# Gate and up products of a SwiGLU layer as Strassen block products, with the hidden tiles kept in DRAM

## The chip, the cores and the metric

The kernel runs on one NeuronCore of a Trainium2 chip. The metric is the device time of one execution, in microseconds (us): the median of three runs.

## The reference

One layer of a hybrid decoder trunk works on 1056 tokens at once: a prompt of 1024 and 32 sample tokens, with shared weights and a model width of 1024. Three token mixers and their output projection come first, then a cross-attention to 256 memory tokens, then the feed-forward part, which is what the change touches:

```python
h = h + mem_attention(rmsnorm(h, W['norm_mem'][l]), mem_k[l], mem_v[l], W['w_mem_q'][l], W['w_mem_o'][l])
u = rmsnorm(h, W['norm_ffn'][l])
h = h + (jax.nn.silu(u @ W['w_ffn_gate'][l]) * (u @ W['w_ffn_up'][l])) @ W['w_ffn_down'][l]
...
y = rmsnorm(h, W['norm_final'])
```

Everything is float32. The hidden width is 2816, 22 tiles of 128 features.

## The kernel before

Activations lie with features on the 128 partitions and tokens along the free side: `h` is eight tiles of 128 x 1056. A main product is done in three passes of float32r matmuls: each operand is split into a high part (a copy rounded to float32r, on ScalarE) and a low part (the rest, a subtraction on VectorE), and `unit` (lines 143 to 153) issues high x high, low x high and high x low for each of `kk` input tiles of 128 features into one PSUM tile of 352 tokens. The tokens are three chunks of 352 (`ch`, `CW`, `NCH`).

TensorE and SyncE (SP, which issues the loads) run in the order of the program text; the order on VectorE (DVE), ScalarE (ACT) and GpSimd (POOL) is made ahead by a scheduler, and each engine then works strictly in that order. Work beside the main products is written as generators: `spawn` starts one, and each `yield n` lets it go on after `n` more half units of main products, counted by `tick` (lines 78 to 95). `strips` (line 120) gives the weight strips in the order of their use, each loaded and split one ahead (`load_split`, `split_into`).

Buffers: `slot` gives one of 28 SBUF tiles of 128 x 1056 values, `slot2` one of 5 more. One PSUM pool, open for the whole kernel, has 3 banks for main products (`mmps`) and 5 for the rest (`smps`).

The work around the change:
- The attention's output product w_o comes in two halves over its input features (`w_o_half`, line 1108): 8 output tiles x 3 chunks x 4 input tiles x 3 matmuls each. As each chunk of the second half leaves PSUM, `residual` adds it to `h` (line 907), `square_into` sums the squares for the norm (ScalarE, then GpSimd at line 221), and `upair` (line 223) writes the high and low part of h times the norm's gain into `u`, 16 tiles.
- `rstd` (line 188) makes the norm's factor per token: sums over features by matmuls with ones, a square root and a Newton step, transposes back onto all partitions (`rbc`). The products don't wait for it, since the factor is applied to their results.
- `hidden` (line 1134) makes a group of 6, 6, 6 or 4 hidden tiles: for each tile and chunk a gate and an up product over 8 input tiles (24 matmuls each), then `evac` (lines 1146 to 1154): gate result x factor, SiLU, up result x factor, their product, and its split into `hh` and `hl`.
- After each of the first three groups the down products over its 6 tiles are added to `h` (lines 1162 to 1167). The last group's down products run over 384, 384 and 288 tokens, each followed by the final norm (`finish`, line 1182) and the store of the output.

## Time and profile before

| what | value |
|---|---|
| runs | 1843.45, 1843.9 and 1845.54 us, median 1843.9 |
| span of the profiled execution, first to last instruction | 1838.8 us |
| instructions | 29217 |
| TensorE, matmuls | 11410, busy 97% of the span |
| VectorE, ScalarE, GpSimd busy | 54%, 38%, 22% |
| DMA | 150.31 MB, mean 82 GB/s |
| mean granted TensorE clock | 0.997 |
| gate and up products | from 1052 us to about 1790, in turns with the down products |

The device time of a run also holds what lies ahead of the first and behind the last instruction; the profiled execution has no separate time of its own on record, so its span stands beside the median of the runs: 5.1 us lie between the two. Busy time of TensorE is the sum of what single matmuls take from their start to their modelled end; successive matmuls overlap, so the distance of their starts tells what one costs in a stream.

### The profile page before, as it was taken

Reading aid. Unit: us, or ns where it says so; the run is one execution under the profiler, and the core shown is the slowest. Engines: PE = TensorE matmul, PEld = TensorE weight load, DVE = VectorE, ACT = ScalarE, POOL = GpSimd, SP = SyncE. Lnnn points to the kernel's source line nnn. Section 1 sums busy time; section 2 is a strip of 40 time slices with the busy share of each in tenths; the row PEclk is TensorE's granted clock in tenths of the full one; section 3 lists DMA queues with packets and bytes.
Section 4 is the critical chain, followed back from the end, with each engine's and each line's share of the span. In section 5 each row is a group of like instructions: output and inputs, shape, how many; then the busy total and the mean of one; then the engine's idle time right before and its main releaser. Section 6 shows DMA issues by size and latency. Waiting matters only on the chain.

```text
span 1838.8 us, 29217 instructions
## 1 busy us (share of the span) xinstructions
PE 1788.8 (97%) x11410; PEld 1739.2 (95%) x11410; DVE 991.9 (54%) x1990; ACT 692.6 (38%) x1403; POOL 412.8 (22%) x516
## 2 busy tenths in 40 slices
PE   8899999999999999999999999999999999999997
PEld 7798888888999999999999999999999999999996
DVE  5888997798745434455575743333333233333345
ACT  6544443577634113355563532211221122211244
POOL 2423557665342222212220400000000000000014
PEclk9999999999999999999999999999999999999999
DMA  9112122341322412234452111111111111111112
GB/s 348 52 60 68 59 57 90 112 134 58 126 84 89 170 58 94 88 121 126 121 180 93 47 47 46 41 48 48 44 46 50 49 36 46 43 52 50 47 47 95
DMA packets 84316, 150.31 MB, mean 82 GB/s; under 512 B 12881, under 2 KB 27857, under 8 KB 84177
## 3 DMA queue, kind: packets, MB, share of 16 engines
q1 hardware_dynamic: 73808, 130.82, 22.2%
q10 hardware_dynamic: 10368, 17.61, 2.7%
q8 instruction: 90, 1.47, 0.3%
q14 instruction: 50, 0.40, 0.1%
HBM read 128.02 MB, written 20.37 MB: 81 GB/s over the span
## 4 chain that ended last, share of the span: by engine, by line
PE 81%; DVE 8%; POOL 3%; issue 3%; ACT 2%; DMA 2%; SPq 0%; ACTq 0%; DVEq 0%; POOLq 0%
PE mm L148 24%; PE mm L149 24%; PE mm L150 24%; DVE cy L498 1%; PE poa L1077 1%; PE pss L1059 1%; POOL seg L570 1%; DVE x L325 1%; PE poz L1008 1%; DVE seg L553 1%; PE pof L688 1%; DVE ul L225 1%; PE pdg L591 1%; PE psa L1008 1%; DVE h L1205 0%
## 5 line engine op out<-in xcount | busy, mean ns | idle before, releaser
L148 PE MATMUL mm<-uh,whi 128*128 128x352 f32 x2016 | 661.7, 328 | 0.8 <-DVE h L907 0.8
L150 PE MATMUL mm<-uh,wlo 128*128 128x352 f32 x2016 | 650.6, 323 | 0.0
L149 PE MATMUL mm<-ul,whi 128*128 128x352 f32 x2016 | 650.6, 323 | 0.0
L148 PEld LDWEIGHTS mm<-uh,whi 128*128 128x128 f32 x2016 | 380.1, 189 | 5.3 <-issue 2.9
L149 PEld LDWEIGHTS mm<-ul,whi 128*128 128x128 f32 x2016 | 380.1, 189 | 2.5
L150 PEld LDWEIGHTS mm<-uh,wlo 128*128 128x128 f32 x2016 | 379.3, 188 | 0.0
L117 ACT ACTIVATE whi<-wraw 128x512 fp32r<-128x512 f32 (+1 forms) x264 | 151.8, 606 | 372.7 <-PE mm L149 340.8
L1218 POOL TENSOR_TENSOR acc_mem<-acc_mem,sq 128x384 f32<-128x384 f32 (+1 forms) x18 | 17.6, 980 | 740.6 <-ACT sq L1216 740.1
L118 DVE TENSOR_TENSOR wlo<-wraw,whi 128x512 fp32r<-128x512 f32 x232 | 158.0, 704 | 18.8 <-ACT whi L117 18.2
L150 PE MATMUL mm<-hh,wlo 128*128 128x352 f32 x432 | 139.9, 324 | 0.0
L148 PE MATMUL mm<-hh,whi 128*128 128x352 f32 x432 | 139.6, 323 | 0.0
L149 PE MATMUL mm<-hl,whi 128*128 128x352 f32 x432 | 139.5, 323 | 0.0
L1151 DVE TENSOR_TENSOR t<-mm,rbc_ffn 128x352 f32<-128x352 f32 x66 | 34.7, 525 | 188.5 <-PE mm L150 188.5
L1167 DVE TENSOR_TENSOR h<-h,mm 128x352 f32<-128x352 f32 x72 | 37.6, 522 | 141.3 <-PE mm L150 141.3
L1153 ACT ACTIVATE hh<-t 128x352 fp32r<-128x352 f32 x66 | 32.9, 498 | 182.1 <-DVE t L1152 182.0
L1149 DVE TENSOR_TENSOR t<-mm,rbc_ffn 128x352 f32<-128x352 f32 x66 | 34.7, 525 | 94.8 <-PE mm L150 94.6
L149 PEld LDWEIGHTS mm<-hl,whi 128*128 128x128 f32 x432 | 81.4, 188 | 0.0
L148 PEld LDWEIGHTS mm<-hh,whi 128*128 128x128 f32 x432 | 81.2, 188 | 0.0
L150 PEld LDWEIGHTS mm<-hh,wlo 128*128 128x128 f32 x432 | 81.1, 188 | 0.0
L952 POOL TENSOR_TENSOR kvlo<-kvraw,kvhi 128x512 fp32r<-128x512 f32 x32 | 41.5, 1296 | 161.3 <-ACT kvhi L951 128.8
L498 DVE SCALAR_TENSOR_TENSOR cy<-raw,cst,cy 128x352 f32<-128x352 f32 (+1 forms) x108 | 72.3, 671 | 7.0 <-ACT cy L496 3.6
L1150 ACT ACTIVATE t<-t 128x352 f32<-128x352 f32 x66 | 32.5, 492 | 109.4 <-DVE t L1149 109.4
(395 smaller groups left out, 3329.3 us busy)
## 6 DMA issues: line engine op xcount, KB each, us to landing
wraw<-w_gu SPq DMA_DIRECT2D x88, 256.0 KB, 2.9
seg<-acs_dram SPq DMA_DIRECT2D x32, 256.0 KB, 3.8
wraw<-w_out SPq DMA_DIRECT2D x32, 256.0 KB, 3.7
kvraw<-kc_d SPq DMA_DIRECT2D x32, 256.0 KB, 2.9
kvraw<-vc_d SPq DMA_DIRECT2D x32, 256.0 KB, 2.8
wraw<-w_down SPq DMA_DIRECT2D x32, 256.0 KB, 2.8
kvw<-w_kv SPq DMA_DIRECT2D x15, 512.0 KB, 7.3
wraw<-w_xbc SPq DMA_DIRECT2D x24, 256.0 KB, 3.1
```

The costliest lines, as they stand in the source:

```text
L117: nc.scalar.activation(hi[:, a:b], raw, AF.Copy)
L118: (second if a else nc.vector).tensor_tensor(lo[:, a:b], raw, hi[:, a:b].bitcast(F32), op=OP.subtract)
L148: nc.tensor.matmul(out, whi[:, a:b], xh[:, cols], start=k == 0, stop=False)
L149: nc.tensor.matmul(out, whi[:, a:b], xl[:, cols], start=False, stop=False)
L150: nc.tensor.matmul(out, wlo[:, a:b], xh[:, cols], start=False, stop=k == kk - 1)
L498: nc.vector.scalar_tensor_tensor(y[:, :n], raw[:, j:j + n], w[j], y[:, :n], op0=OP.mult, op1=OP.add)
L952: eng.tensor_tensor(lo, src, hi.bitcast(F32), op=OP.subtract)
L1008: nc.tensor.matmul(pr, diag[:, k * 512 + b * 2 * ST:k * 512 + (b + 1) * 2 * ST], pair[z][:, k], start=b + k + z == 0, stop=b + k + z == NB ...
L1149: nc.vector.tensor_tensor(t1, pg, rbc[:, ch(c)], op=OP.mult)
L1151: nc.vector.tensor_tensor(t2, pu, rbc[:, ch(c)], op=OP.mult)
L1153: nc.scalar.activation(hh[:, ch(c)], t2, AF.Copy)
L1167: nc.vector.tensor_tensor(h[m][:, ch(c)], h[m][:, ch(c)], p, op=OP.add)
```

## The change

The gate and up products are done by Strassen's scheme with seven block products and shared sums (Winograd's form). The two matrices of a pair of hidden tiles (2 x 128 features) and the two halves of the 1024 input features make the 2 x 2 blocks of the left side; the right side is cut the same way by input features and by tokens: two halves `s` of 528 tokens (`TH`). The tokens of each half are again cut in two quarters of 264 (`HB`), and index `c` (0 or 1) takes one quarter from each half; all of it is done for c = 0 and for c = 1 apart.

- `sides(c)` makes the right-hand sides: the normed tokens times gain and factor, four sums and differences, and the high and low parts of all seven, for four input tiles: 14 `slot` tiles for each c, so all 28. Two products share tiles `x2`, `x3`, `x4`.
- `lefts` loads the strips of a pair of tiles, makes the sums s1 to s4 and splits the seven left-hand sides, in four lists. `ahead_of` prepares none ahead in the first block and two lists ahead later.
- `product` issues 4 input tiles x 3 matmuls of 264 columns. The seven products fall into four PSUM tiles of two banks (`G[0]` to `G[3]`, three buffers); products 0 and 2, 1 and 3, 4 and 6 add up in the same tile, and the partial sum is read in between (`after`). The first gate block and the last up block run all seven products for c = 0 and then for c = 1 (`by_part`); the others run each product for both.
- `gate` and `up` combine the results, apply SiLU and multiply, and the four pieces of two hidden tiles are stored to `hid_dram` on ScalarE's DMA queue.
- The second half of w_o runs over quarters: both halves `s` of c = 0 for all 8 output tiles, then c = 1, with all its weights split once and held (`hold`). Behind c = 0 `sides(0)` is spawned, behind c = 1 `sides(1)`. `h` is stored to `h_dram`.
- The down products come after all hidden tiles. `load_hidden` reads a hidden tile back and splits it (ScalarE and VectorE, 1056 columns), six ahead of the first product and one per output tile after that; `h` is loaded again. Their matmuls stay as they were; the last eight weight strips are loaded behind the third group.
- PSUM is given out by three pools in turn, the second with six banks for `G` and two for the rest.

The diff, cut to its core:

```diff
+TH = T // 2
+HB = TH // 2
...
+        lists += [(w_o[0, m], 512) for m in range(8)]
+        yield from one_ahead(lists, mixers)
...
+    hid_dram = dr.tile([P, FT, T], F32, name="hid_dram")
...
+    def both(t, c):
+        return t.rearrange("p (s t) -> p s t", s=2)[:, :, c * HB:(c + 1) * HB]
...
+    def rstd2(c):
+        pv = smps(name="pv")
+        cuts = [(2 * s + i, s * TH + c * HB + i * P, P) for s in range(2) for i in range(2)]
+        cuts += [(4 + s, s * TH + c * HB + 2 * P, HB - 2 * P) for s in range(2)]
+        for i, a, n in cuts:
+            nc.tensor.matmul(pv[:n, i:i + 1], acc[:, a:a + n], ones[:, :1], start=True, stop=True)
...
+        newton(r, v, q)
+        yield 2
+        for s in range(2):
+            pb = smps(name="pb")
+            a0 = s * TH + c * HB
+            for i, a, n in cuts:
+                if a0 <= a < a0 + HB:
+                    nc.tensor.transpose(pb[:, a - a0:a - a0 + n], r[:n, i:i + 1].to_broadcast([n, P]), ident[:n, :n])
+            nc.scalar.activation(rbc[:, a0:a0 + HB], pb[:, :HB], AF.Copy)
...
+    def sides(c, n0):
+        yield n0
+        yield from rstd2(c)
+        un = {}
+        def normed(k):
+            un[k] = fp.tile([P, 4, HB], F32, tag="ar", name=nm("un"), bufs=4)
+            for j in range(2):
+                nc.scalar.activation(un[k][:, 2 * j:2 * j + 2], both(h[k + 4 * j], c), AF.Copy, scale=cc("gffn", k + 4 * j))
+                (nc.gpsimd if j else nc.vector).tensor_tensor(un[k][:, 2 * j:2 * j + 2], un[k][:, 2 * j:2 * j + 2], both(rbc, c),
+                                                              op=OP.mult)
+        def pair(t, q, n, src):
+            hi = t[:, q * HB:(q + n) * HB].rearrange("p (s t) -> p s t", s=n)
+            lo = t[:, (q + n) * HB:(q + 2 * n) * HB].rearrange("p (s t) -> p s t", s=n)
+            nc.scalar.activation(hi, src, AF.Copy)
+            nc.vector.tensor_tensor(lo, src, hi.bitcast(F32), op=OP.subtract)
+            return [(quarters(t, q + i), quarters(t, q + n + i)) for i in range(n)]
+        normed(0)
+        for k in range(4):
+            if k < 3:
+                normed(k + 1)
+            u4 = un[k]
+            tt = fp.tile([P, 4, HB], F32, tag="as", name=nm("tt"), bufs=2)
+            if k % 2 == 0:
+                first = slot(F32R, "x1")
+            X["B11", k, c] = pair(first, k % 2 * 2, 1, u4[:, 0:1])[0]
+            nc.vector.tensor_tensor(tt[:, 0:2], u4[:, 1::2], u4[:, 0:2], op=OP.subtract)
+            nc.vector.tensor_tensor(tt[:, 2], u4[:, 3], tt[:, 0], op=OP.subtract)
+            nc.vector.tensor_tensor(tt[:, 3], u4[:, 2], tt[:, 2], op=OP.subtract)
+            X["T2", k, c], X["T4", k, c] = pair(slot(F32R, "x2"), 0, 2, tt[:, 2:4])
+            X["B21", k, c], X["B22", k, c] = pair(slot(F32R, "x3"), 0, 2, u4[:, 2:4])
+            X["T1", k, c], X["T3", k, c] = pair(slot(F32R, "x4"), 0, 2, tt[:, 0:2])
...
+    def hold():
+        m = len(held)
+        if m % 2 == 0:
+            hold.at = [(wp if m < 4 else fp).tile([P, DM], F32R, tag=t if m < 4 else "b" + t, name=nm(t), bufs=2) for t in ("whi", "wlo")]
+        hi, lo = (t[:, m % 2 * 512:m % 2 * 512 + 512] for t in hold.at)
+        split_into(w_o[1, m], 512, hi, lo)
+        held.append((hi, lo))
+    hold()
+    for c in range(2):
+        for m in range(8):
+            while len(held) < min(m + 2, 8):
+                hold()
+            for s in range(2):
+                cols = slice(s * TH + c * HB, s * TH + (c + 1) * HB)
+                p = mmps()[:, :HB]
+                unit(p, held[m], op1, cols, 4)
+                nc.vector.tensor_tensor(h[m][:, cols], h[m][:, cols], p, op=OP.add)
+            if m:
+                sq = fp.tile([P, 2, HB], F32, tag="sq2", name=nm("sq"), bufs=2)
+                nc.scalar.activation(sq, both(h[m], c), AF.Square)
+                nc.gpsimd.tensor_tensor(both(acc, c), both(acc, c), sq, op=OP.add)
+            else:
+                nc.scalar.activation(both(acc, c), both(h[m], c), AF.Square)
+            if c:
+                nc.scalar.dma_start(h_dram[:, m, :], h[m])
+        if c == 0:
+            spawn(sides(0, 4))
+    drain()
+    ps_.close()
+    sm_bufs = 2
+    ps_ = ExitStack()
+    ps = ps_.enter_context(tc.tile_pool(name="ps2", bufs=2, space=PSUM, reuse_waits="tile"))
+    spawn(sides(1, 1))
...
+    def lefts(pairs):
+        raws = []
+        def load(i):
+            r = [fp.tile([P, DM], F32, tag="ar", name=nm("ar"), bufs=4, padded_shape=[P, T]) for _ in range(2)]
+            for k in range(2):
+                for t, src in zip(r, pairs[i]):
+                    nc.sync.dma_start(t[:, k * 512:k * 512 + 512], src[:, k * 512:k * 512 + 512])
+            raws.append(r)
+        load(0)
+        for i in range(len(pairs)):
+            (a11, a12), (a21, a22) = [(t[:, :512], t[:, 512:]) for t in raws.pop(0)]
+            if i + 1 < len(pairs):
+                load(i + 1)
+            sa, sb = (fp.tile([P, DM], F32, tag="as", name=nm("as"), bufs=2, padded_shape=[P, T]) for _ in range(2))
+            s1, s2, s3, s4 = sa[:, :512], sa[:, 512:], sb[:, :512], sb[:, 512:]
+            nc.gpsimd.tensor_tensor(s1, a21, a22, op=OP.add)
+            nc.gpsimd.tensor_tensor(s3, a11, a21, op=OP.subtract)
+            nc.vector.tensor_tensor(s2, s1, a11, op=OP.subtract)
+            nc.vector.tensor_tensor(s4, a12, s2, op=OP.subtract)
+            for n, srcs in enumerate(((a11, s2), (a12, s3), (s1, a22), (s4,))):
+                pool, b = (fp, "b") if n % 2 else (wp, "")
+                hi, lo = (pool.tile([P, DM], F32R, tag=b + t, name=nm(t), bufs=2) for t in ("whi", "wlo"))
+                for j, src in enumerate(srcs):
+                    a = slice(j * 512, j * 512 + 512)
+                    nc.scalar.activation(hi[:, a], src, AF.Copy)
+                    nc.vector.tensor_tensor(lo[:, a], src, hi[:, a].bitcast(F32), op=OP.subtract)
+                yield [(hi[:, j * 512:j * 512 + 512], lo[:, j * 512:j * 512 + 512]) for j in range(len(srcs))]
...
+    def ahead_of(gen):
+        got = []
+        for x in gen:
+            got.append(x)
+            while len(got) > lead[0]:
+                yield from got.pop(0)
...
+    PRODUCTS = ("B11", 0, True), ("T2", 1, True), ("B21", 0, False), ("T3", 1, False), ("T1", 2, True), ("T4", 3, True), ("B22", 2, False)
+    NF2 = FT // 2
+    blocks = ahead_of(lefts([(w_gu[j, 2 * f], w_gu[j, 2 * f + 1]) for f in range(NF2) for j in range(2)]))
...
+    def product(i, w, G, c, kk):
+        xb, g, begins = PRODUCTS[i]
+        whi, wlo = w
+        for k in range(kk):
+            a, b = k * P, k * P + P
+            xh, xl = X[xb, k, c]
+            out = G[g][:, c, :HB]
+            nc.tensor.matmul(out, whi[:, a:b], xh, start=begins and k == 0, stop=False, skip_group_check=True)
+            nc.tensor.matmul(out, whi[:, a:b], xl, start=False, stop=False, skip_group_check=True)
+            nc.tensor.matmul(out, wlo[:, a:b], xh, start=False, stop=k == kk - 1, skip_group_check=True)
+        tick()
...
+    def strassen(kk, after, by_part):
+        G = {}
+        if by_part:
+            ws = [next(blocks) for _ in range(7)]
+            for c in range(2):
+                for i in range(7):
+                    g = PRODUCTS[i][1]
+                    if g not in G:
+                        G[g] = ps.tile([P, 2, 512], F32, tag="st", name=nm("st"), bufs=3)
+                    product(i, ws[i], G, c, kk)
+                    after(i, slice(c, c + 1), G)
+                G = {}
+            return
+        for i in range(7):
+            g = PRODUCTS[i][1]
+            if g not in G:
+                G[g] = ps.tile([P, 2, 512], F32, tag="st", name=nm("st"), bufs=3)
+            w = next(blocks)
+            for c in range(2):
+                product(i, w, G, c, kk)
+            after(i, slice(0, 2), G)
...
+        def gate(i, cs, G):
+            m1, u2, u3 = s22[:, cs], s12[:, cs], s21[:, cs]
+            at = lambda g: G[g][:, cs, :HB]
+            vec = nc.vector.tensor_tensor
+            if i == 0:
+                nc.scalar.activation(m1, at(0), AF.Copy)
+            elif i == 1:
+                vec(u2, m1, at(1), op=add)
...
+        strassen(4, gate, f == 0)
+        lead[0] = 2
...
+                nc.gpsimd.tensor_tensor(s22[:, cs], s22[:, cs], m1, op=mul)
...
+        strassen(4, up, f == NF2 - 1)
+        for n, t in enumerate(ga):
+            nc.scalar.dma_start(hid_dram[:, 2 * f + n // 2, n % 2 * TH:(n % 2 + 1) * TH], t.rearrange("p c t -> p (c t)"))
...
+        def load_hidden():
+            f = len(hids)
+            hi, lo = slot(F32R, "hh"), slot(F32R, "hl")
+            nc.sync.dma_start(lo.bitcast(F32), hid_dram[:, f, :])
+            nc.scalar.activation(hi, lo.bitcast(F32), AF.Copy)
+            nc.vector.tensor_tensor(lo, lo.bitcast(F32), hi.bitcast(F32), op=OP.subtract)
+            hids.append((hi, lo))
+        weights = one_ahead([(w_down[m, :, f0 * P:(f0 + nf) * P], nf * P) for f0, nf in FGROUPS[:-1] for m in range(8)])
+        for _ in range(FGROUPS[0][1]):
+            load_hidden()
+        h = [slot2(F32, "h") if m < 5 else slot(name="h") for m in range(8)]
+        nc.sync.dma_start(h[0], h_dram[:, 0, :])
...
         for f0, nf in FGROUPS[:-1]:
-            hid = hidden(f0, nf)
             for m in range(8):
                 w = next(weights)
+                if f0 == 0 and m < 7:
+                    nc.sync.dma_start(h[m + 1], h_dram[:, m + 1, :])
+                if len(hids) < min(f0 + nf + 6, FT):
+                    load_hidden()
                 for c in range(NCH):
                     p = mmps()
-                    unit(p, w, hid, ch(c), nf)
+                    unit(p, w, hids[f0:f0 + nf], ch(c), nf)
                     nc.vector.tensor_tensor(h[m][:, ch(c)], h[m][:, ch(c)], p, op=OP.add)
```

## Rows read from the trace of the kernel before

**Rows 1.** The page, part 1: busy us (share of the span), instructions of each engine
```profile
PE 1788.8 (97%) x11410; PEld 1739.2 (95%) x11410; DVE 991.9 (54%) x1990; ACT 692.6 (38%) x1403; POOL 412.8 (22%) x516
```

**Rows 2.** The page, part 4: the chain that ended last, by engine and line
```profile
PE 81%; DVE 8%; POOL 3%; issue 3%; ACT 2%; DMA 2%; SPq 0%; ACTq 0%; DVEq 0%; POOLq 0%
PE mm L148 24%; PE mm L149 24%; PE mm L150 24%; DVE cy L498 1%; PE poa L1077 1%; PE pss L1059 1%; POOL seg L570 1%; DVE x L325 1%; PE poz L1008 1%; DVE seg L553 1%; PE pof L688 1%; DVE ul L225 1%; PE pdg L591 1%; PE psa L1008 1%; DVE h L1205 0%
```

**Rows 3.** Busy time by stage: length, engines, granted clock, DMA share, GB/s
```profile
1018.00:1064.00 46.00, 44.62 (x279) 43.45 (x277) 34.26 (x62) 25.77 (x51) 19.31 (x22) 1.00 0.16 52
...
1150.00:1250.00 100.00, 100.00 (x623) 100.00 (x622) 33.93 (x65) 16.48 (x34) 0.00 (x0) 1.00 0.15 46
...
14.00:16.00 2.00, 2.00 (x18) 2.00 (x17) 0.61 (x1) 1.06 (x1) 0.00 (x0) 1.00 1.02 405
```

**Rows 4.** Timeline, TensorE, key projection, 20 matmuls apart: start, us, instruction
```profile
33.00 0.28 PE L148 MATMUL pk<-mhi,kvh 128*128 128x256 f32 x1
...
35.36 0.28 PE L150 MATMUL pk<-mhi,kvl 128*128 128x256 f32 x1
```

**Rows 5.** Timeline, TensorE, last tokens, 33 matmuls apart
```profile
1816.84 0.30 PE L149 MATMUL mm<-hl,wd 128*128 128x288 f32 x1
...
1821.20 0.30 PE L149 MATMUL mm<-hl,wd 128*128 128x288 f32 x1
```

**Rows 6.** Timelines, VectorE and ScalarE, the norm of chunk 0 ahead of the feed-forward
```profile
1058.08 0.15 DVE L200 TENSOR_SCALAR nv<-pv 128x2 f32<-128x2 f32 x1
...
1059.37 0.16 DVE L184 TENSOR_TENSOR nr<-nr,nq 128x3 f32<-128x3 f32 x1
...
1060.14 0.47 ACT L207 ACTIVATE rbc_ffn<-pb 128x352 f32<-128x352 f32 x1 [0.21 <-PE pb L206]
```

**Rows 7.** Groups by line and form, VectorE: count, busy us, mean ns, idle before
```profile
L118 DVE TENSOR_TENSOR wd<-wraw,wd 128x512 fp32r<-128x512 f32 x8 | 5.4, 692 | 1.6 <-ACT wd L117 1.6
...
L118 DVE TENSOR_TENSOR wlo<-wraw,whi 128x256 fp32r<-128x256 f32 x24 | 10.1, 419 | 0.0
...
L1152 DVE TENSOR_TENSOR t<-t,t 128x352 f32<-128x352 f32 x66 | 34.6, 524 | 4.6
...
L221 DVE TENSOR_TENSOR acc<-acc,sq 128x1056 f32<-128x1056 f32 x3 | 3.7, 1246 | 0.0
...
L907 DVE TENSOR_TENSOR h<-h,mm 128x352 f32<-128x352 f32 x72 | 36.9, 516 | 53.6 <-PE mm L150 53.6
```

**Rows 8.** Groups by line and form, ScalarE
```profile
L117 ACT ACTIVATE whi<-wraw 128x512 fp32r<-128x512 f32 x240 | 144.5, 626 | 372.7 <-PE mm L149 340.8 <-PE mm L150 12.8 <-issue 5.3
...
L882 ACT ACTIVATE yh<-yr 128x1056 fp32r<-128x1056 f32 x8 | 8.6, 1085 | 29.0 <-DMA yr<-ya_dram 21.9 <-PE mm L149 7.1
```

**Rows 9.** Groups by line and form, GpSimd
```profile
L1218 POOL TENSOR_TENSOR acc_mem<-acc_mem,sq 128x384 f32<-128x384 f32 x12 | 12.5, 1044 | 733.8 <-ACT sq L1216 733.6
...
L1218 POOL TENSOR_TENSOR acc_mem<-acc_mem,sq 128x288 f32<-128x288 f32 x6 | 5.1, 854 | 6.8 <-ACT sq L1216 6.5
```

**Rows 10.** Timelines, VectorE and then GpSimd, the norm of the first 384 tokens
```profile
1799.75 5.71 DVE L1205 TENSOR_TENSOR h<-h,rbc_ffn 128x384 f32<-128x384 f32 x5 [0.76 <-ACT rbc_ffn L1202]
...
1799.80 3.96 POOL L1205 TENSOR_TENSOR h<-h,rbc_ffn 128x384 f32<-128x384 f32 x3 [1.25 <-ACT rbc_ffn L1202]
1803.72 1.32 POOL L1218 TENSOR_TENSOR acc_mem<-acc_mem,sq 128x384 f32<-128x384 f32 x1
```

**Rows 11.** Timeline, TensorE, near the kernel's start, 12 matmuls apart
```profile
11.30 0.41 PE L148 MATMUL pk<-mhi,kvh 128*128 128x256 f32 x1
...
13.86 0.41 PE L148 MATMUL pk<-mhi,kvh 128*128 128x256 f32 x1
```

**Rows 12.** DMA issues: count, KB each, median us from issue to landing
```profile
h_dram<-h ACTq DMA_DIRECT2D x8, 528.0 KB, 3.0
...
h<-h_dram SPq DMA_DIRECT2D x8, 528.0 KB, 5.8
```

More of the change, by code (lines that the diff above doesn't have):

```diff
@@ L1115, in w_o_half @@
                     unit(p, w, op, ch(c), 4)
[L1116 to L1124 removed]
+                    residual(m, c, p, None, False, None, None, last=False)
+        w_o_first(op0)
         drain()
@@ new lines, in hybrid_step @@
+    held = []
+    def hold():
[25 more added lines that the diff above has]
+            spawn(sides(0, 4))
@@ new lines, in hybrid_step @@
+    drain()
+    fp_.close()
+    ps_.close()
+    sm_bufs = 5
+    ps_ = ExitStack()
+    ps = ps_.enter_context(tc.tile_pool(name="ps3", bufs=4, space=PSUM, reuse_waits="tile"))
+    with tc.tile_pool(name="fq", bufs=1, reuse_waits="tile") as fp:
+        hids = []
+        def load_hidden():
[10 more added lines that the diff above has]
+        nc.sync.dma_start(h[0], h_dram[:, 0, :])
```

113 lines of the change are left out of this document (66 added, 47 removed).

## The prediction

> **What bounds the kernel now.** Read first how busy each engine is: TensorE 97% of the span, VectorE 54% [rows 1]. The chain that ended last says the same, 81% of it is TensorE and nearly three quarters are the three matmul lines of `unit` [rows 2]. The table by stage shows where this holds without a gap: in the gate and up stretch (1150 to 1250 us) TensorE is busy all the time at full clock, VectorE a third of it, and the DMA moves 46 GB/s [rows 3]. So the feed-forward is worth what its matmuls cost, and whatever runs beside them is free while it fits. How many matmuls fit into 100 us is the number to take from there: 623, so one starts every 0.1605 us. The 0.32 us that a row gives as a matmul's own time overlaps the next one and is of no use here.
>
> The span is 1838.8 us and the median of the runs 1843.9; the 5.1 us around the span are taken as unchanged, and the sum is made on the span.
>
> **Gate and up products.** Before: 22 hidden tiles x 2 matrices x 3 chunks x 8 input tiles x 3 matmuls = 3168 of 352 columns, x 0.1605 = 508.5 us. After: 11 pairs of tiles x 2 x 7 block products x 2 halves x 4 x 3 = 3696 of 264 columns. No row has 264. Its neighbours are the 256 columns of the key projection, (35.36 - 33.00)/20 = 0.118 us [rows 4], and the 288 of the last tokens, (1821.20 - 1816.84)/33 = 0.132 [rows 5]; both ends as a price would save 72 or 21 us. The three widths lie on a line (0.00044 us a column), so I take 0.118 + 8 x 0.00044 = 0.1215, and 3696 x 0.1215 = 449.1: **59.4 us less**. The Trainium skill, page TensorE: Matmul & The Clock Gate, section Back-to-back issue gap, gives the gap of a lone stream as columns over 2.4 plus 2.5 ns; by that the saving would be 3168 x 149.2 - 3696 x 112.5 ns = 56.9 us. The rows lie 9 to 11 ns above that rule, and the sum goes by the rows.
>
> The second half of the w_o products goes from 288 matmuls of 352 to 384 of 264: 46.7 - 46.2 = **0.5 us more**. Its old gaps (46.0 - 44.6 us in 1018 to 1064 [rows 3]) go in part: **1 us less**.
>
> **The entry into the new stage** is what decides. Before, the operands `u` were split as each w_o tile left PSUM, with the norm's factor applied afterwards on the results; the products began at once. Now nothing of a half's seven right-hand sides can be made before that half's norm is known. Let A be the moment at which the factor of half 0 lies on all partitions: 2.9 us of yielded units behind the last w_o product of half 0, then four steps as in the old chain, which took 2.5 us from its first VectorE step to the copy [rows 6], and the squares ahead of them: some 7 us into the w_o products of half 1. These take 23.3 us, so 16.3 are left.
>
> VectorE's prices: 128x512 from SBUF 0.69, x1056 1.25, x256 0.42, x352 0.52 [rows 7], hence 0.71 for 528 and 0.43 for 264 columns. From A to the start of half 1's products it must do, nearly all in this order:
> - sides of half 0: four times (5 of 528 and 3 of 264) = 19.4
> - 11 remaining w_o adds x 0.43 = 4.7
> - the first seven left-hand sides: 9 x 0.69 = 6.2 (their raw tiles share four buffers with the normed tokens, so they can't come much earlier)
> - five results of half 0 = 2.2, the norm of half 1 = 1.3
> - sides of half 1 up to the last B11, which begins: 19.4 - 3.7 = 15.7.
>
> Together 49.5 us. ScalarE's share lies beside it: 28 us of copies for the sides, 4.4 for the left sides, some 10 for the rest, by 0.63 for 512 and 1.09 for 1056 columns [rows 8]. GpSimd runs 15 instructions in this time (8 mults, 5 square sums, 2 weight sums), about 1.33 us each by the line through 384 and 288 columns [rows 9], 19.9 us. Are they free? The norm at the end shows both engines full: five VectorE mults of 384 columns, 0.55 us each by the line of [rows 7], took 5.71 us beside GpSimd's three and one, 3.96 and 1.32 us [rows 10], so 2.96 us were added by four instructions of 1.04, 0.71 of their own time. That gives 14; I take 12, since adds out of PSUM keep 0.52 us beside GpSimd [rows 7] and cover some. Ends: 0 and 19.9.
>
> So half 1's products start at A + 61.5 and end 10.2 later (84 x 0.1215), where an unhindered TensorE would be through at A + 16.3 + 0.7 + 20.4 = A + 37.4. **The entry costs 71.7 - 37.4 = 34.3 us**, between 22.3 (GpSimd free) and 42.2 (fully in turn). TensorE idles in two pieces, ahead of each half.
>
> **Clock.** A gap of that length is not in the rows of this stage; at the start of the kernel, after gaps, 256-column matmuls ran at (13.86 - 11.30)/12 = 0.213 us, at the lower of the clock's two levels [rows 11], for some microseconds. Half 1's 84 products at that level throughout would cost 8.2 us more; the end of VectorE's work covers part. **3 us** (0 to 8).
>
> **The steady stage.** A block of seven products takes 168 x 0.1215 = 20.4 us; VectorE has 9 x 0.69 + 5 to 7 x 0.71 = 10 to 11 us in it, ScalarE 8, GpSimd 3 to 5: they fit. But PSUM now holds sums that are read midway: products 0 and 2, 1 and 3, 4 and 6 share a bank, so product i+2 waits until the result of i was read. Between lies one product, 2.9 us, against 0.71 for the read and what is queued ahead of it on the in-order engine. Two weight splits ahead of it still fit; a third, or one held up by GpSimd, does not. **3 us** over 22 blocks (0 to 10). The four stores of a pair sit on ScalarE's queue behind the last mults; behind them is the next block's first copy, needed 2.9 us later. They land in 3.0 us [rows 12]. Nothing waits for them until the down products.
>
> **The down products** keep their matmuls. Their operands are loaded (22 x 528 KB) and split, 1.09 + 1.25 us each, instead of being split in place. In the last block half 0's operands free 14 buffers 10.2 us early, enough for seven loads; at 405 GB/s [rows 3] six take 8 us, 5.8 us each alone [rows 12]. Behind them on SP's queue wait the first residual and the first weight strips, behind the last of them the split. If that cover went, a load and a split (8 us) would show. New PSUM pool: its first tiles wait for the last reads. **1.5 us** (0 to 5).
>
> Sum: -59.4 + 0.5 - 1 + 34.3 + 3 + 3 + 1.5 = -18.1. Span 1820.7, time **1826 us**. The lows give -59.4 + 0.5 - 1.4 + 22.3 = -38, 1806; the highs -59.4 + 0.5 + 42.2 + 8 + 10 + 5 = +6, 1850.
>
> **Rivals.**
> - *GpSimd and VectorE take full turns* (0.20): the entry is 42.2 us, the time 1834. For it: with 0.71 the row is nearer to full turns than to none, and ScalarE and VectorE work in pairs, each waiting for the other. Against: the row itself. The Trainium skill, page SBUF — State Buffer, section Who interferes with whom, states that a VectorE instruction with two SBUF inputs and a GpSimd instruction that reads SBUF exclude each other, one blocking the other fully. The row shows 71% of that.
> - *The entry is short* (0.13): the left-hand sides are made before A, in the half-idle VectorE of half 0, and GpSimd's work falls into gaps. The entry is 22.3, less up to 6: 1800 to 1810. Against it: the shared buffers.
> - *The banks hold TensorE up in each block* (0.14): the read of a half-finished sum stands on VectorE behind a burst of weight splits. A burst of three is 2.1 us, with GpSimd's sum in between 3.4, so 1 to 2 us a block and 22 to 44 in all. From 1.1 us a block the kernel is slower than before; at 1.6 it is 1826 - 3 + 35 = 1858. For it: VectorE is in order, and its order is fixed ahead. Against: it has half its time free.
> - *The loads of hidden tiles wait for the last store* (0.08): were the whole scratch tensor one dependency, then store 3.0, load 5.8 and split 2.3 show at the entry of the down products, with the clock some 13 us: 1838.
>
> **The numbers.** My forecast has 0.45. A measurement of this kernel can tell about 0.2%, 3.7 us, from no change. Faster: 0.42 of the forecast's 0.45, 0.13 of full turns, all 0.13 of the short entry, 0.04 of the waiting loads: 0.72. Within 0.2%: 0.03 + 0.04 + 0.03 + 0.01 = 0.11. Slower: 0.03 + 0.13 + 0.01 = 0.17. The range runs from 1804, in the short entry, to 1850, the forecast's top, and leaves out most of the bank rival.
>
> **What would show it.** Right: matmuls of 264 columns 0.1215 us apart with TensorE busy throughout the blocks; two idle stretches of 10 to 25 us ahead of the two halves of the first block, ended by VectorE; a lower granted clock there and nowhere else; no gap at the down products above 2 us. Wrong: idle time of TensorE released by VectorE or ScalarE in each block (banks); a first block without the long idle stretches; a pitch off 0.1215 by over 0.004, which is 15 us.

## The result, and the profile after

| | runs | median us | ratio to before, 95% interval |
|---|---|---|---|
| before | 4 | 1844.04 (1843.45 to 1845.54) | |
| changed | 4 | 1826.53 (1825.80 to 1827.52) | 0.9908, 0.9894 to 0.9922 |

The change saves 17.5 us. The profiled execution of the changed kernel took 1827.24 us, its span is 1825.3. The two spans lie only 13.5 us apart, because the profiled execution of before was one of its shorter ones, as far as its span tells (the run with the DMA setting, below).

The page of the changed kernel, parts 1 and 4, answers to [rows 1] and [rows 2]:

```profile
PE 1747.0 (96%) x12043; PEld 1694.2 (93%) x12043; DVE 1091.0 (60%) x2043; ACT 743.5 (41%) x1445; POOL 533.2 (29%) x584
...
PE 79%; DVE 10%; issue 3%; POOL 3%; ACT 2%; DMA 2%; SPq 0%; ACTq 0%; DVEq 0%; POOLq 0%
```

TensorE still bounds the kernel. It is 42 us less busy, more than the time fell: the rest stands idle somewhere. A stretch of steady blocks (columns as in [rows 3]) shows that it is not there:

```profile
1150.00:1250.00 100.00, 100.00 (x822) 100.00 (x821) 50.87 (x73) 29.06 (x49) 22.82 (x14) 1.00 0.24 78
```

822 matmuls of 264 columns in 100 us, one every 0.1217 us, at full clock and without a gap. What remains idle around the new stage is named by the waits of TensorE from 1000 to 1125 us (engine, line <- what it waited for: us in all, times, longest):

```profile
PE mm L151 <- DVE h L1218: 11.5, 2, 9.4
PE st L1290 <- DVE tm L1341: 6.1, 1, 6.1
PE st L1291 <- DVE x L1179: 3.1, 2, 1.9
PE pb L1153 <- DVE nr L187: 2.6, 2, 1.4
```

L151 with `mm` is a w_o product, L1218 its addition to `h`, L1290 and L1291 are lines of `product`, L1341 is VectorE's read of the fifth gate product, L1179 a low part of a right-hand side. The largest wait is inside w_o, which the prediction had run through. The same stretch by time:

```profile
1030.00:1040.00 10.00, 8.57 (x70) 7.92 (x69) 4.21 (x12) 4.61 (x8) 3.20 (x3) 1.00 0.14 57
1040.00:1050.00 10.00, 2.18 (x18) 1.97 (x17) 10.00 (x14) 2.13 (x4) 4.88 (x3) 0.79 0.01 1
1050.00:1060.00 10.00, 6.32 (x27) 6.01 (x28) 9.97 (x17) 5.22 (x10) 3.05 (x2) 0.50 0.66 219
1060.00:1070.00 10.00, 10.00 (x73) 9.98 (x73) 7.93 (x14) 3.54 (x6) 6.39 (x5) 0.86 0.48 157
1070.00:1080.00 10.00, 8.78 (x68) 7.91 (x68) 4.97 (x11) 6.70 (x13) 3.57 (x3) 1.00 0.53 213
1080.00:1090.00 10.00, 6.42 (x49) 5.61 (x47) 8.29 (x18) 4.90 (x9) 3.59 (x2) 1.00 0.00 0
1090.00:1100.00 10.00, 4.67 (x22) 4.25 (x22) 9.93 (x16) 6.74 (x13) 3.14 (x2) 0.66 0.01 2
1100.00:1110.00 10.00, 7.56 (x30) 6.78 (x31) 9.17 (x17) 5.86 (x12) 2.68 (x2) 0.52 0.29 92
```

VectorE (the third pair) is full from 1040 to 1060 and from 1090 on, and half idle from 1070 to 1080. TensorE has two holes, each followed by a stretch at a clock of about 0.5. Its timeline names their ends:

```profile
1032.24 1.18 PE L1141 MATMUL pv<-ones,acc_mem 128*128 128x1 f32 x12
1036.52 1.09 PE L1153 MATMUL pb<-msk,nr 128*128 128x128 f32 x6 [1.43 <-DVE nr L187]
1051.62 0.59 PE L151 MATMUL mm<-oh,whi 128*128 128x264 f32 x1 [9.44 <-DVE h L1218]
1056.69 0.59 PE L151 MATMUL mm<-oh,whi 128*128 128x264 f32 x1 [2.07 <-DVE h L1218]
...
1073.54 0.36 PE L1290 MATMUL st<-x,whi 128*128 128x264 f32 x1 [0.61 <-DVE h L1218]
1075.65 1.23 PE L1141 MATMUL pv<-ones,acc_mem 128*128 128x1 f32 x12
...
1081.88 1.09 PE L1153 MATMUL pb<-msk,nr 128*128 128x128 f32 x6 [1.14 <-DVE nr L187]
1093.63 0.59 PE L1290 MATMUL st<-x,whi 128*128 128x264 f32 x1 [6.07 <-DVE tm L1341]
```

Read from the top: the norm of half 0 (`pv`, `pb`), then VectorE makes half 0's sides, and the w_o additions queue behind them, so that w_o stops for 9.4 us for want of free PSUM tiles. w_o ends late, so does the norm of half 1 (second `pv` and `pb`), for which VectorE in turn stands idle. The last row is not yet half 1: it is the seventh product of half 0, which adds up in the PSUM tile of the fifth and waits until VectorE has read the fifth's sum. The fifth was through at 1086; VectorE, making half 1's sides, comes to the read 7 us later:

```profile
1092.54 0.70 DVE L1172 TENSOR_TENSOR un<-un,rbc_ffn 128x528 f32<-128x528 f32 x1
1093.16 0.42 DVE L1341 TENSOR_TENSOR tm<-tm,st 128x264 f32<-128x264 f32 x1
```

Half 1's products begin twelve matmuls behind it, at 1096.44, and end at 1115.72; their first two still wait for half 1's sides (L1179, 1.9 and 1.2 us).

For comparing runs, call **the way** the time from the first matmul of w_o's second half (1005.95 us here) to VectorE's first read of an up product (1121.84): 115.9 us. Unhindered it would be 73.9: w_o 384 x 0.1217 = 46.7, a hand-over of 0.7, two halves of the gate block 20.4, two up products for both halves 5.8, and 0.3 for the read. So the entry costs **42 us**, with the lower clock. The 73.9 is a sum, no run has it. From that read to the last matmul of the up products, 424.1 us pass in the changed kernel and in every run of it and of its edits below but the one with a half's sides left out (e3).

The second place is the start of the down products. From 1545.94, the start of the last up matmul, to 1549.27 TensorE starts nothing; the waits there, and ScalarE's timeline ahead of them:

```profile
PE mm L151 <- ACT whi L121: 3.0, 1, 3.0
PE mm L153 <- DVE wlo L122: 0.8, 1, 0.8
```

```profile
1544.99 1.43 ACTq L1379 DMA_DIRECT2D hid_dram<-tm  x2
1546.46 1.08 ACT L1395 ACTIVATE hh<-hl 128x1056 fp32r<-128x1056 f32 x1 [3.96 <-POOL fv L1434]
1547.24 0.33 ACTq L1379 DMA_DIRECT2D hid_dram<-tm  x1
1547.62 1.08 ACT L1395 ACTIVATE hh<-hl 128x1056 fp32r<-128x1056 f32 x1
1548.61 1.44 ACT L121 ACTIVATE whi<-wraw 128x512 fp32r<-128x512 f32 x3
```

ScalarE works in order: the issues of the last stores and the copies of the last two hidden tiles (L1395) stand ahead of the copy of the first w_down strip (L121), which is what TensorE waits for. The hidden loads themselves were no matter: they were issued from 1526.51 us on, and part 6 of the page gives them 4.1 us and the stores 2.1 us to land. The granted clock fell here too: it is 0.50 from 1550.90 to 1554.30.

### The profile page after: what moved, and what is told of

The parts are those of the page before. It is cut to its first block, busy times and chain, and to the rows that moved or that the text cites. A ratio compares the mean times of both kernels' runs of the same rounds, so it can differ in the third digit from the quotient of the medians.

```text
span 1825.3 us, 30861 instructions
## 1 busy us (share of the span) xinstructions
PE 1747.0 (96%) x12043; PEld 1694.2 (93%) x12043; DVE 1091.0 (60%) x2043; ACT 743.5 (41%) x1445; POOL 533.2 (29%) x584
## 4 chain that ended last, share of the span: by engine, by line
PE 79%; DVE 10%; issue 3%; POOL 3%; ACT 2%; DMA 2%; SPq 0%; ACTq 0%; DVEq 0%; POOLq 0%
PE mm L151 15%; PE mm L153 15%; PE mm L152 15%; PE st L1291 8%; PE st L1292 8%; PE st L1290 8%; DVE cy L502 2%; PE poa L1081 1%; PE pss L1063 1%; DVE x L329 1%; POOL seg L574 1%; PE poz L1012 1%; DVE x L1179 1%; PE psa L1012 1%; DVE seg L557 1%
## 5 line engine op out<-in xcount | busy, mean ns | idle before, releaser
L1290 PE MATMUL st<-x,whi 128*128 128x264 f32 x1232 | 353.3, 287 | 7.7 <-DVE tm L1341 6.1
L1291 PE MATMUL st<-x,whi 128*128 128x264 f32 x1232 | 352.7, 286 | 3.1 <-DVE x L1179 3.1
L1292 PE MATMUL st<-x,wlo 128*128 128x264 f32 x1232 | 353.0, 287 | 0.5 <-DVE wlo L1264 0.5
L151 PE MATMUL mm<-uh,whi 128*128 128x352 f32 x960 | 319.9, 333 | 0.0
L153 PE MATMUL mm<-uh,wlo 128*128 128x352 f32 x960 | 310.5, 323 | 0.0
L152 PE MATMUL mm<-ul,whi 128*128 128x352 f32 x960 | 310.2, 323 | 0.0
L1290 PEld LDWEIGHTS st<-x,whi 128*128 128x128 f32 x1232 | 234.3, 190 | 8.8 <-DVE tm L1341 6.3
L1291 PEld LDWEIGHTS st<-x,whi 128*128 128x128 f32 x1232 | 233.8, 190 | 3.6 <-DVE x L1179 3.6
L1292 PEld LDWEIGHTS st<-x,wlo 128*128 128x128 f32 x1232 | 234.2, 190 | 0.9 <-DVE wlo L1264 0.9
L151 PEld LDWEIGHTS mm<-uh,whi 128*128 128x128 f32 x960 | 181.1, 189 | 4.3 <-issue 1.9
L152 PEld LDWEIGHTS mm<-ul,whi 128*128 128x128 f32 x960 | 181.6, 189 | 2.5
L153 PEld LDWEIGHTS mm<-uh,wlo 128*128 128x128 f32 x960 | 181.0, 189 | 0.0
L121 ACT ACTIVATE whi<-wraw 128x512 fp32r<-128x512 f32 (+1 forms) x176 | 100.3, 596 | 176.1 <-PE mm L152 143.6
L151 PE MATMUL mm<-hh,whi 128*128 128x352 f32 x432 | 140.3, 325 | 3.0 <-ACT whi L121 3.0
L151 PEld LDWEIGHTS mm<-hh,whi 128*128 128x128 f32 x432 | 81.6, 189 | 3.3 <-ACT whi L121 3.3
```

Of the source, the lines that this page charges most:

```text
L121: nc.scalar.activation(hi[:, a:b], raw, AF.Copy)
L151: nc.tensor.matmul(out, whi[:, a:b], xh[:, cols], start=k == 0, stop=False)
L152: nc.tensor.matmul(out, whi[:, a:b], xl[:, cols], start=False, stop=False)
L153: nc.tensor.matmul(out, wlo[:, a:b], xh[:, cols], start=False, stop=k == kk - 1)
L1290: nc.tensor.matmul(out, whi[:, a:b], xh, start=begins and k == 0, stop=False, skip_group_check=True)
L1291: nc.tensor.matmul(out, whi[:, a:b], xl, start=False, stop=False, skip_group_check=True)
```

## The experiments

One table first; "start" is the first matmul of w_o's second half, "stop" the time from the start of the last up matmul to that of the first down matmul, all from the profiled execution; the medians and ratios are over all executions of a run.

| run | median us | ratio to before, 95% | start | the way | stop |
|---|---|---|---|---|---|
| changed kernel | 1826.53 | 0.9894 to 0.9922 | 1005.95 | 115.9 | 3.33 |
| e2, adds between the sides | 1827.21 | 0.9898 to 0.9925 | 1004.00 | 116.6 | 3.33 |
| e3, one half's sides | 1803.92 | 0.9775 to 0.9803 | 1006.00 | 96.2 | 0.12 |
| e4, multiplies on VectorE | 1822.92 | 0.9865 to 0.9898 | 1009.67 | 110.5 | 3.34 |
| e5, early norm | 1826.77 | 0.9895 to 0.9926 | 1003.51 | 114.2 | 3.33 |
| e6, strip first | 1823.18 | 0.9867 to 0.9904 | 1010.13 | 115.5 | 0.12 |
| e7, early norm and adds | 1824.04 | 0.9881 to 0.9910 | 1005.96 | 111.7 | 3.34 |
| e8, all of these | 1818.35 | 0.9852 to 0.9881 | 1007.36 | 112.4 | 0.13 |
| e9, left sides first | 1820.11 | 0.9850 to 0.9892 | 1009.48 | 112.2 | 0.12 |
| e10, multiplies and strip | 1816.02 | 0.9834 to 0.9868 | 1004.62 | 110.4 | 0.12 |
| e11, GpSimd idle | 1822.05 | 0.9865 to 0.9902 | 1004.53 | 110.6 | 3.34 |

The start differs by 6.6 us between executions that are alike up to there, so a single execution says little of a few microseconds; the way and the stop do (e6 leaves the way untouched and repeats it within 0.4 us). The edits shift line numbers by a few.

### e1: the kernel before with the changed kernel's DMA setting

The full diff also sets the size of the dynamic DMA scratch. The kernel before, with that alone:

```diff
-    nc = bacc.Bacc("TRN2", target_bir_lowering=False, num_devices=1)
+    nc = bacc.Bacc("TRN2", target_bir_lowering=False, num_devices=1, dynamic_dma_scratch_size=1024)
```

> The kernel before with one other setting of the change alone: the scratch for DMA descriptors made on the chip is cut to 1024. The changed kernel's time around its span is about 2 us (1827.2 against a span of 1825.3), before it was about 5. Theory 1, the setting shortens what lies around the span: 3 us less than before, the span the same within 1 us. Theory 2, the time around the span hangs on something else in the new program: the same time as before within 1 us.

Measured: 1843.96 us against 1843.39, ratio 0.9995 to 1.0014. The setting does nothing that could be told from noise. Its profiled execution has 1841.06 us and a span of 1839.3: 1.8 us around the span, and 1.7 to 1.9 in every other execution of the kernel before that has both numbers (1.7 to 3.1 in the changed kernel and its edits). The 17 executions of the kernel before in this comparison reach from 1840.3 us (span 1838.5, mean granted clock 0.997) to 1847.8 (span 1846.1, clock 0.993). So the span of 1838.8 that the prediction started from belongs to an execution of some 1840.6 us, 3.3 under the median; the "5.1 us around the span" were 1.8 and this difference.

### e2: w_o's additions between the sides

```diff
             X["T1", k, c], X["T3", k, c] = pair(slot(F32R, "x4"), 0, 2, tt[:, 0:2])
+            if c == 0 and k < 3:
+                yield 6
```

> The changed kernel, but the sides of half 0 are emitted in four parts, six half units of w_o products apart, so that the w_o adds between them get their place on VectorE. Theory 1, the entry is long because the adds stand behind the sides on VectorE, TensorE stops inside the w_o products (9.4 and 2.1 us), falls to the lower clock, and the norm of half 1 comes late: the two stops fall below 3 us in all, the sides of half 1 begin some 10 us earlier, and the time is 8 to 12 us less than the changed kernel's, 1815 to 1818. Theory 2, VectorE's sum of work alone sets the end of the entry, whatever the order: within 2 us of 1826.5.

Measured: 1827.21 us, the way 116.6. TensorE's waits in the entry:

```profile
PE mm L151 <- DVE h L1220: 7.4, 5, 2.0
PE st L1292 <- DVE tm L1343: 6.1, 1, 6.1
```

The 11.5 us for which w_o waited became 7.4 us in five pieces, the longest 2.0, and nothing came of it: the 6.1 us ahead of half 0's last product stayed as they were. w_o ended 5.9 us earlier, yet VectorE's first multiply by half 1's factor came 77.5 us behind the start, as in the changed kernel. Order alone is not it.

### e3: the sides of one half only

Left out: the norm and the right-hand sides of half 1; its products use those of half 0.

```diff
-    spawn(sides(1, 1))
...
-            xh, xl = X[xb, k, c]
+            xh, xl = X[xb, k, 0]
```

> The changed kernel without the second half's norm and right-hand sides: the products of half 1 take the sides of half 0 again (this part of the computation is left out). Theory 1, in the entry TensorE waits above all for VectorE's sides of half 1: the wait of 6.1 us and the smaller ones behind it, as well as the lower clock there, go; half 1's products follow half 0's at once; 16 to 20 us less, 1807 to 1811. Theory 2, the left-hand sides or the results bound the first block: at most 5 us less.

Measured: 1803.92 us, the way 96.2: 19.7 us shorter. TensorE's waits in the same stretch:

```profile
PE mm L151 <- DVE h L1218: 11.5, 2, 9.4
PE pb L1153 <- DVE nr L187: 1.4, 1, 1.4
PE st L1289 <- DVE tm L1334: 1.3, 1, 1.3
```

The hole in w_o stays to the tenth, the wait ahead of half 0's last product is gone (the 1.3 us stand ahead of its fourth). So of the 42 us of the entry, 20 go with half 1's norm and sides, and 22 remain without them (96.2 - 73.9). The rest of its 22.6 us comes from the down products, for which half of the operand buffers were free all along. That moved the hidden tiles' copies and splits into the blocks, which took 426.3 us instead of 424.1, and there, between 1400 and 1500 us, TensorE was idle for 1.46 us, waiting once for VectorE and once for ScalarE. A wait of this kind is what the bank rival named, a burst that falls into a block; in the changed kernel's steady blocks none does.

### e4: the norm's multiplies on VectorE

```diff
-                (nc.gpsimd if j else nc.vector).tensor_tensor(un[k][:, 2 * j:2 * j + 2], ...
+                nc.vector.tensor_tensor(un[k][:, 2 * j:2 * j + 2], ...
```

> The changed kernel with the eight mults of the normed tokens that ran on GpSimd moved to VectorE. VectorE gets 8 x 0.71 = 5.7 us more work in the entry, and GpSimd's eight instructions of 1.33 us no longer stand beside it. Theory 1, a GpSimd instruction takes 0.71 to 0.76 of its own time from VectorE (0.94 to 1.01 us): 2 us less, about 1824. Theory 2, both take full turns: 5 us less, 1821 to 1822. Theory 3, GpSimd is free: 5 to 6 us more, 1832.

Measured: 1822.92 us, the way 110.5, 5.4 us shorter, although VectorE got eight instructions more. In the changed kernel, GpSimd's multiplies, and what VectorE does meanwhile:

```profile
1038.11 6.77 POOL L1172 TENSOR_TENSOR un<-un,rbc_ffn 128x528 f32<-128x528 f32 x4 [5.97 <-ACT rbc_ffn L1154]
```

```profile
1038.07 2.47 DVE L1172 TENSOR_TENSOR un<-un,rbc_ffn 128x528 f32<-128x528 f32 x2 [1.61 <-ACT rbc_ffn L1154]
1040.46 1.55 DVE L1179 TENSOR_TENSOR x<-un,x 128x264 fp32r<-128x264 f32 x1
1041.93 1.80 DVE L1191 TENSOR_TENSOR tt<-un 128x528 f32<-128x528 f32 x1
1043.65 1.79 DVE L1172 TENSOR_TENSOR un<-un,rbc_ffn 128x528 f32<-128x528 f32 x1
1045.37 0.42 DVE L1192 TENSOR_TENSOR tt<-un,tt 128x264 f32<-128x264 f32 x1
```

Undisturbed, VectorE's instructions of 528 and 264 columns follow each other by 0.62 and 0.34 us (1047.02, 1047.64, 1048.26 further on in this timeline). Four of the one and one of the other are 2.8 us; they took 7.3. Four GpSimd instructions of 1.33 us added 4.5 us, 0.84 of their own time. Over the whole entry, the two stretches shown at e10, which has this edit too, give the price of all eight: with eight multiplies more VectorE is busy for 50.78 + 12.13 = 62.9 us, without them for 46.66 + 19.18 = 65.8. The eight are 8 x 0.62 = 5.0 us of work, so on GpSimd they had cost VectorE 2.9 + 5.0 = 7.9 us, 1.0 each, 0.74 of their time. The other half of the gain is idle time of VectorE, 9.3 us instead of 11.9. So theory 2 fits the time, but the price of a single multiply is nearer to theory 1.

### e5: half 1's norm ahead of the first product

On top of e4:

```diff
-        yield 2
+        if c == 0:
+            yield 2
...
-    spawn(sides(1, 1))
+    late = sides(1, 0)
+    next(late)
+    heapq.heappush(queue, (now[0] + next(late), next(order), late))
```

(and a `yield 1` behind `rstd2` for half 1).

> Edit: the norm's multiplies all on VectorE (as in the run that moved them), and half 1's norm issued on TensorE ahead of the first product instead of behind it and two more. Theory 1 (VectorE's total work sets the end of the entry; with the multiplies moved it still stood idle for some 6.7 of the 50 us behind 1050 us, 2.9 of them while it waited for the norm's sums and 1.6 for the factor): the factor of half 1 lies on all partitions some 3 us earlier, half 1's products start 2 to 4 us earlier, about 1819 to 1821 us. Theory 2 (the norm is not what holds VectorE back; the sums only come when the last square is added): the products of half 0 now stand behind the norm on TensorE and nothing is gained, 1822 to 1825 us.

Measured: 1826.77 us, the way 114.2: nothing gained, as theory 2 has it, and by the way worse than e4. TensorE's waits in the entry, the two of the norm last:

```profile
PE mm L151 <- DVE h L1221: 12.2, 2, 11.0
PE st L1295 <- DVE tm L1346: 8.7, 1, 8.7
PE pb L1154 <- DVE nr L187: 4.0, 2, 2.5
PE pv L1141 <- POOL acc_mem L1225: 2.7, 1, 2.7
```

Half 1's factor came no earlier (VectorE's first multiply by it 74.8 us behind the start, 74.1 in e4), since the last square has to be added first; and ScalarE, in order, held three copies of left-hand sides back for 3.7 us behind a step of the norm. Half 0's products stood behind both, and the last of them (L1346 is the read that it waits for) began 94.1 us behind the start instead of 90.0.

### e6: the first w_down strip ahead of the hidden tiles

In the changed kernel alone:

```diff
-        weights = one_ahead([(w_down[...], nf * P) for ...])
+        strip = [(w_down[...], nf * P) for ...]
+        weights = one_ahead(strip[1:], 0, load_split(*strip[0], nc.vector))
```

> Edit to the changed kernel alone: the first w_down strip is loaded and split ahead of the six hidden tiles instead of behind them. Theory 1 (the 3.3 us of idle TensorE at the down products come from ScalarE's order: the stores' issues and the copies of the last hidden tiles stand ahead of the first strip's copy): the idle stretch falls from 3.3 us to below 1, and the time from 1826.5 to about 1823.5. Theory 2 (the stretch is set by the last hidden tiles or by the PSUM pool's change): the strip is ready earlier, but the first product waits for something else as long, 1826 us.

Measured: 1823.18 us, 3.35 less than the changed kernel, and the stop fell from 3.33 to 0.12 us. ScalarE's copies of the first strip now run 7 us ahead of the last up product (at 1549.75 in this execution):

```profile
1542.69 0.94 ACT L121 ACTIVATE whi<-wraw 128x512 fp32r<-128x512 f32 x2
```

In place of the stop, TensorE waits twice for the low parts of the last hidden tiles:

```profile
PE mm L151 <- DVE hl L1395: 1.0, 2, 0.6
```

Theory 1 holds by the stop. That the median fell by as much is partly chance: the four executions reach from 1819.49 to 1826.24 us.

### e7: early norm and additions between the sides

e5 with the yields of e2.

> Edit: as the run with the early norm and all multiplies on VectorE, and between the four input tiles of half 0's sides the w_o adds go first (the yields of six units, which alone changed nothing). Theory 1 (VectorE's total decides; the yields brought nothing alone because the norm of half 1 still stood behind the first product, which waited for VectorE): w_o ends earlier, the factor of half 1 lies ready before VectorE has done half 0's sides, and VectorE has no idle time until half 1's products: another 2 to 4 us on top of the early norm, 1815 to 1819 us. Theory 2 (the order does not matter at all): as the early norm alone, 1819 to 1823 us.

Measured: 1824.04 us, the way 111.7: no better than e4 alone. w_o ended 7 us earlier than in e4, but `pv` then waited 6.3 us for GpSimd's last sum of squares. GpSimd and VectorE in this run at 1043 us:

```profile
1042.77 7.26 POOL L1227 TENSOR_TENSOR acc_mem<-acc_mem,sq 128x528 f32<-128x528 f32 x2 [10.62 <-ACT sq L1226]
```

```profile
1044.47 0.70 DVE L1194 TENSOR_TENSOR tt<-un 128x528 f32<-128x528 f32 x1
1045.71 0.70 DVE L1182 TENSOR_TENSOR x<-un,x 128x528 fp32r<-128x528 f32 x1
```

Here it is GpSimd that stands: two additions of 1.33 us took 7.26, while VectorE ran at its own pace.

### e8: all of these together

> Edit: all of these together: multiplies on VectorE, early norm, yields, first down strip ahead. If the gains are those of separate places they add: the time of the run with norm and yields less 3 us, 1812 to 1816 us, faster than both kernels. If the down strip's copy is paid elsewhere on ScalarE, no better than that run.

Measured: 1818.35 us, the way 112.4, the stop 0.13. The strip's gain of the stop adds to the others, but the time lies above the 1812 to 1816 expected, as e7 had not gained what was expected of it.

### e9: left-hand sides ahead of the norm

e8, with `first = [[next(blocks) for _ in range(7)]]` ahead of half 1's norm and the last two squares of half 1 added on VectorE.

> Edit: as the run with all edits together, and the first seven left-hand sides stand in the program ahead of half 1's norm (before, ScalarE and VectorE held their copies and subtractions back behind the norm's steps, 3.3 us of idle VectorE and 5.7 of ScalarE), and the squares of the last two w_o tiles are added on VectorE, not GpSimd (TensorE waited 6.3 us for GpSimd's last sum). Theory 1 (VectorE's own work sets the end of the entry, and what is left to gain is its idle time ahead of half 1's factor): the way from the first w_o product of the second half to the first up result, 112.4 us in the run with all edits, falls to 106 to 109; 1813 to 1816 us. Theory 2 (the factor of half 1 can come no earlier, the subtractions only change places): 112 us, 1818 us.

Measured: 1820.11 us, the way 112.2: theory 2. `pv` waited 3.8 us instead of 6.3, but the scheduler put the subtractions of the left-hand sides between the norm's steps, and `pb` waited 5.4 where it had waited 2.5.

### e10: multiplies and strip alone

> Edit: multiplies on VectorE and the first down strip ahead, with neither the early norm nor the yields. Theory 1 (the early norm costs as much TensorE time ahead of half 0's products as it gains behind them; the two edits that gained do so in separate places): the way to the first up result 110.5 us as with the multiplies alone, the idle stretch at the down products 0.1 us, 1817 to 1820 us. Theory 2 (early norm and yields are worth 4 to 5 us, as the difference of the medians with and without the strip suggests): 1821 to 1823 us.

Measured: **1816.02 us, ratio 0.9834 to 0.9868**, 27.5 us under the kernel before on its chip (1843.47) and some 10 under the changed kernel, without early norm or yields. The way is 110.4, the stop 0.12. It is the fastest of the complete kernels. Theory 1 by the way and the stop; the time lies 1 us below its range. The medians of e4 and e6 fell by 3.6 and 3.4 us, which does not add up to the 10.5 here; way and stop together give 8.7. By stretches, the changed kernel first, then this one: from half 0's factor on all partitions to half 0's last product, and from there to the end of half 1's block:

```profile
1038.03:1093.63 55.60, 35.67 (x245) 33.45 (x243) 46.66 (x79) 26.23 (x50) 23.82 (x16) 0.81 0.30 107
1093.63:1115.80 22.17, 18.03 (x97) 16.83 (x98) 19.18 (x32) 12.35 (x26) 5.38 (x4) 0.70 0.19 60
```

```profile
1036.70:1094.30 57.60, 32.57 (x245) 30.89 (x243) 50.78 (x97) 29.51 (x56) 14.20 (x9) 0.84 0.30 103
1094.30:1108.90 14.60, 14.30 (x97) 14.14 (x98) 12.13 (x22) 9.00 (x19) 2.70 (x2) 0.82 0.27 91
```

VectorE does more instructions (97 against 79) in the first stretch and has less left for the second. Half 0's last product starts 2 us later by this count (TensorE waits 11.7 us here for VectorE's read of the fifth), and from there TensorE runs through half 1 without a further wait: its sides are nearly done. Whether that read, put ahead of half 1's sides on VectorE, would gain something in either kernel was not tried.

### e11: nothing for GpSimd in the entry

On top of e4, without the strip: the squares of the second quarters (L1222) and the sums s1, s3 of the first weight pair on VectorE as well.

> Edit: multiplies, the squares' sums of the second quarters and the two weight sums of the first block all on VectorE, so that GpSimd has nothing to do in the entry. VectorE gets 9 more instructions of about 0.7 us, 6.4 us in all. Theory 1 (the engines exclude each other fully, so that an instruction of 1.33 us on GpSimd costs VectorE 1.33 us): the entry is at least as short as with the multiplies alone, 106 to 110.5 us to the first up result, 1819 to 1823 us. Theory 2 (only 0.71 of GpSimd's time is lost, and part of it in VectorE's idle time): the moved work costs more than it frees, 112 to 115 us, 1825 to 1828 us.

Measured: 1822.05 us, the way 110.6 as in e4. Nine more instructions of 0.7 us on VectorE cost nothing. That fits theory 1, but part of them falls into VectorE's idle time, so it does not show a price of its own.

## Why the prediction was right, and where it was not

- **The time** (1826 forecast, 1826.53 measured): the saving forecast for the medians, 17.9 us, was 17.5. The mechanism, cheaper matmuls in all blocks against one long entry, is what the trace shows; no rival took its place. But several terms were off and offset each other, and that the sum came within 1 us is luck.
- **The start of the sum** failed as a step: "5.1 us around the span" are 1.8 (e1). As a difference of medians the sum is unharmed; started from its own execution, it would have given 1822.5.
- **Pitch**: 0.1215 forecast, 0.1217 measured, 58.7 us saved instead of 59.4. The line through two neighbouring widths was good to 0.2%.
- **The entry** was mis-sized: 34.3 + 3 us forecast, 42 measured. VectorE was the right engine, and its work nearly right: with contention 61.5 us up to half 1 and 5.9 more behind it (3.7 of sides, 2.2 of results) were forecast, 67 in all; it was busy for 46.66 + 19.18 = 65.8 (the two stretches of the changed kernel in e10). Two slips cancel in this. The price per instruction was its duration, 0.71 and 0.43 us, where successive ones follow by 0.62 and 0.34: the mistake that the prediction avoided for TensorE. And the list was too short: in the two stretches VectorE makes 17 instructions of left-hand sides, not 9, since those of the next pair fall into them too. The contention was priced about right: GpSimd's multiplies took 0.74 of their own time from VectorE (e4), 0.71 was taken.
- What was missed is **VectorE's idle time**: in the two stretches together it stood for 77.8 - 65.8 = 11.9 us. The step "nearly all in this order" took it for one queue without a gap; in fact half 1's norm needs the end of w_o, and w_o stood behind half 0's sides. Then sums, factor, copy, and VectorE waits: 4.5 us for the sums and the factor, and 4.2 for w_o's own late products. Also half 0's factor lay ready 8.7 us into half 1 of w_o instead of 7. With A = 1038.03, half 1's products began at A + 58.4 (61.5 forecast) and ended at A + 77.7 (71.7 forecast, 74.7 with the clock): not their start was late but their block was long, 19.3 us instead of 10.2.
- **The places** were wrong with it: two idle stretches of 10 to 25 us ahead of the two halves were named; there is one of 9.4 us inside w_o and one of 6.1 ahead of half 0's last product, with waits inside half 1's block. What the prediction listed as 11 cheap additions decided where TensorE stops first. The second stop is what its bank rival described, a product that waits for the read of a half-finished sum, but in the entry, where VectorE is full, and not in the blocks. e2, e5, e7 and e9 move the holes about: the way stays between 110 and 117 us.
- **Clock**: named for half 1's block, and the profile shows it for both holes: 0.22 us between w_o's matmuls from 1051.6 to 1062.7, and 0.66 and 0.52 in the windows from 1090 to 1110. Behind each hole TensorE waits for VectorE anyway for part of it, so its share of the 42 us was not taken apart. "There and nowhere else" failed as well: behind the stop at the down products the clock was 0.50 for 3.4 us.
- **Steady blocks**: 3 us forecast, none measured; the order of splits and reads on VectorE, half idle there, never held a bank.
- **Down products**: 1.5 us forecast, "no gap above 2 us"; 3.33 + 0.80 measured. The step went through the loads and SP's queue and had named the stores on ScalarE's queue, yet put no price on what follows them there: the first strip's copy. e6 took the stop away and its time.
- **Full turns** (0.20): its entry of 42.2 us is the measured 42, but for another reason. The eight multiplies took 7.9 us from VectorE by e10's stretches, not the 10.6 of full turns, and VectorE's 11.9 us of idle time were in no rival. The page's rule of exclusion (the Trainium skill, SBUF — State Buffer, Who interferes with whom) is borne out in part: 0.84 in the first four multiplies and 0.74 over all eight are near the 0.71 of [rows 10], and in e7 it is GpSimd that is held up.

The terms as measured, -58.7 + 0.5 - 1 + 42 + 0 + 4.1, make -13; the two profiles, each counted from the start of w_o's second half (1003.66 before, 1005.95 after), differ by 835.14 - 819.35 = 15.8. What the terms leave out goes both ways. In the kernel before, the 27 small matmuls of the norm took TensorE 2.7 us, and the gate and up products took 509.8 us by their starts, 1.3 more than the sum has. In the changed kernel the lower clock behind the stop costs some 1 us: the down products took 264.3 us from the first to the last, 263.1 in e6 and e10.

## What to carry to other kernels

Price a stream of instructions by the distance of their starts, on every engine, and take one execution's span as one execution. Where a stage begins with work that one in-order engine must do first, look for what of the *previous* stage runs through the same engine: its small reads of PSUM stop TensorE, and the next stage's inputs come late in turn. Moving them about only moved the stops here (e2, e5, e7, e9); less work on the engine shortened the stage (e4). A helper is no help where its instructions hold up the bottleneck: eight instructions taken from GpSimd and given to the full VectorE made the entry 5 us shorter.

## What the runs showed of the hardware

- Contention between VectorE and GpSimd goes either way. In the changed kernel, behind half 0's factor, four GpSimd multiplies took 6.77 us instead of 5.3 and added 4.5 us to VectorE; in e7, where VectorE ran back to back, two GpSimd additions took 7.26 us instead of 2.7 and VectorE lost nothing until the end. What decides between the two was not tried.
- Behind a hole of 9.4 us, TensorE's matmuls of 264 columns came 0.22 us apart for 11 us (with one more wait of 2.1 us among them), at a granted clock of 0.50, the lower of its two levels, before they came 0.12 apart again.
- The time ahead of a stage that no edit touches moved by up to 6.6 us from one execution to the next (1003.5 to 1010.1 us), while the 424.1 us of the blocks behind it repeated to 0.02.
